# Out-projection weights split beside the narrow products; mix, q and k loaded at other places; the end reordered

## The chip, the cores and the metric

The kernel runs on one core of a Trainium2 chip. The metric is the device time of one execution in microseconds (us); lower is better. The kernel before took 1015.14 us, the median of three runs (1014.92 to 1019.17).

## What is computed

One decoder layer on 1024 positions of width 1024, in float32. The input is normed (`pre_norm_g`) and multiplied by `w_in` (1024 x 7184). The columns of the result feed two groups of heads. The first group is eight heads of differential attention: two causal softmax maps per head, the second subtracted with the weight `lam`, times values of width 128, then a norm and a gate. The second is four heads of gated linear attention (GLA), with decays from a low-rank product, also normed and gated. Both are put side by side and multiplied by `w_out` (2048 x 1024); the result is normed and added to the input:

```
z = einsum('bsd,de->bse', rms_norm(x, pre_g), w_in)
oa = rms_norm(diff_attention(qa, ka, va, lam), subln_g) * (1 - lam_init) * silu(ga)
ob = rms_norm(gla_chunked(qb, kb, vb, log_a), gla_g) * silu(gb)
y = einsum('bse,ed->bsd', concatenate([oa, ob], -1), w_out)
return x + rms_norm(y, post_g)
```

## The kernel before

**Split operands.** Most products are made from float32 operands split in two: ACT copies a tile to a rounded high part, DVE subtracts that from the tile and keeps the low part, and TensorE makes three products, high by high, high by low and low by high. So each weight tile that is used costs one ACT copy and one DVE subtraction. That holds for the weights of the in-projection (L284 with L285, and L327 with L329) and for `w_out`.

**The in-projection in seven products.** Each 1024 x 1024 by 1024 x n product is cut into two by two blocks and made with seven block products instead of eight, numbered 1 to 7; DVE makes the block sums. `order` (L193 to L206) is a list, written by hand, of all these steps, and `go(n)` (L681) does the next n of them: it prepares the weights of the coming steps, issues the matmuls, drains PSUM and hands the result out. There are two kinds of step. A *wide* step (`step_wide`, L442; kinds VB and VA, the values of both attentions) has 24 matmuls of 512 columns into four PSUM banks. A *narrow* step (`step`, L469; a pair `(p, n)` of two 128-column groups) has 12 matmuls into one bank. All 28 wide steps come early, right behind steps 1 and 2 of the first three pairs. Those three pairs keep a bank each through the whole wide stage, so that the wide steps work with five of the eight banks. In a wide step of kind n = 2, 5, 3 or 4 `take_values` (L420) drains the banks: DVE adds (L425), for VA ACT copies the high part (L432) and DVE subtracts (L433), and SP stores the tiles. The staging tiles `st` have four buffers.

**The out-projection's weights.** `w_out` is loaded, split and stored back to DRAM in 32 pieces of 128 x 512, so that later stages can load finished high and low parts. A piece is one load `wo_raw` (L678), an ACT copy `wo_hi`, a DVE subtraction into `wo_raw` and the stores on SP's queue. `wo_raw` has one buffer, so the next load waits until the last store of the piece before has landed. Before the change 17 pieces are done behind wide steps (`wo_wide`, L661: ACT L668, DVE L669, two half tiles each, stores L670 and L671) and 15 behind narrow ones (`wo_step`, L649: ACT L653, DVE L655, stores L657). In the narrow stage a piece's load and its split stand behind steps of certain numbers n, two pieces in seven steps.

**Around the narrow stage.** The low-rank decays are computed between narrow steps: `decay(g)` (L785) is a chain through PE, ACT, DVE, a scan and ACT again. From step (8, 5) on, pieces of GLA are mixed in behind each step (`fill`). `LEAD` steps before the end of `order`, GLA is finished, the first head's q, k and ks (k with its two parts exchanged) are loaded, then the first split `w_out` tiles (`weights(e)`, L1022, into the buffers of h11, h12, s1 and h22, two e to a buffer pair, each free once the last product that reads it is done) and the first two tiles `m_hi`, `m_lo` of GLA's finished part of the mix (`mix`, L1044, into the buffers of s2).

**The attention stage.** Three streams are merged by a fixed plan of costs (`merge`, L1070): scores with softmax (`all_scores`, L1202), values (`all_values`, L1310) and out-projection products that are ready early (`out_early`, L1377). Query blocks go from 7 down to 0 in each head. q, k and ks are tiles of 128 x 2 x 512 in halves 0 and 1. All have one buffer, but for half 0 of k and ks, which have a second one for odd heads (L991). The next head's tiles are loaded behind query block 4. In `values`, `turn` transposes a block of the weights and splits it (ACT L1235, DVE L1236) and `times` (L1239) multiplies.

**The end.** `last_part` (L1354) splits the last head's part of a row tile of the mix (ACT L1357, DVE L1358) and `last_times` multiplies it; `early_ends` (L1462) does that for the first two row tiles, `prime` for the others.

**Queues.** Matmuls are kept in program order. The order on the other engines is set by a scheduler that runs when the program is built. Nearly all DMAs are issued by SP, in one queue; a DMA also waits until the eighth DMA before it on that queue has landed.

## Time and profile before

| what | value |
|---|---|
| median of three runs | 1015.14 us |
| the profiled execution: time, span | 1020.25 us, 1018.6 us |
| mean TensorE clock granted | 0.985 of full |
| busy PE / DVE / ACT / POOL | 973.4 / 740.4 / 594.6 / 141.2 us |
| DMA, mean over the span | 216 GB/s |

The profile page lists the busy time of each engine, the span in 40 slices, the DMA queues and the costliest groups of instructions. Further views of the trace give a table by stretches of time (with the clock granted to TensorE, PEclk), waits by who ended them, instructions in order of time, and the chain of work that ended last. PE is busy in 96% of the span, but a busy PE is not always at its full rate: matmuls overlap in the pipeline, so the count of matmuls in a stretch tells more than its busy time. The stages lie as follows: the input's norm and transposes to 14 us, wide steps with the first narrow ones to 216 us, narrow steps to 649 us (GLA from about 380 to 611 us), attention to about 975 us, then the end.

### The profile page before, as it was taken

To read this page: it belongs to the slowest core of one execution; us is meant where nothing else is said; L and a number is where in the kernel's file an instruction comes from. 1 tells how busy PE (TensorE), PEld (TensorE's weight loads), DVE (VectorE), ACT (ScalarE), POOL (GpSimd) and SP (SyncE) were. 2 spreads that over 40 slices of the span, in tenths; PEclk is the share of its full clock that TensorE was granted. 3 is DMA by queue.
4 is the path that set the end of the run, shared out by engine and by line. 5 is a ranking of instruction groups with operands and counts; after the bars stand their busy time and mean duration, and the time that the engine had idled before them with its cause. 6 is when DMAs were issued, how large, how long until landed. Compare 5 with 4: busy or idle time off the path is not lost.

```text
span 1018.6 us, 14888 instructions
## 1 busy us (share of the span) xinstructions
PE 973.4 (96%) x4866; PEld 814.5 (80%) x4866; DVE 740.4 (73%) x1467; ACT 594.6 (58%) x1169; POOL 141.2 (14%) x153
## 2 busy tenths in 40 slices
PE   6998999799999999999999999899999999999987
PEld 4876767678778888888888888788888888788866
DVE  6995457589879966777777776477777777687745
ACT  8642233335537646765567775256666677677764
POOL 5410000100000000000000000022231222333332
PEclk9999999899989999999999999999999999999999
DMA  9556646586775674566876658995765679964567
GB/s 335 192 144 211 215 154 217 185 233 176 215 244 196 222 265 166 186 197 209 247 207 186 197 186 237 413 328 186 221 202 190 207 251 342 314 179 84 165 198 153
DMA packets 159101, 220.38 MB, mean 216 GB/s; under 512 B 16320, under 2 KB 88256, under 8 KB 158928
## 3 DMA queue, kind: packets, MB, share of 16 engines
q1 hardware_dynamic: 154992, 212.10, 64.5%
q0 software_dynamic: 4032, 7.34, 4.6%
q8 instruction: 38, 0.62, 0.3%
q14 instruction: 39, 0.32, 0.1%
HBM read 133.93 MB, written 88.60 MB: 218 GB/s over the span
## 4 chain that ended last, share of the span: by engine, by line
PE 64%; DMA 12%; DVE 4%; ACT 3%; issue 3%; SPq 1%; POOL 0%; DVEq 0%; ACTq 0%; POOLq 0%
PE x L117 14%; PE z L117 9%; PE ypart L117 9%; PE y L117 8%; PE sc L117 5%; PE po L117 4%; PE yps L117 4%; PE gpo L117 3%; PE v L117 2%; DMA wo_raw<-in_w_out_dram 2%; PE wtr L120 2%; DMA wo_lo<-wo_d 1%; DMA ks<-k_d 1%; DMA q_d<-qk_st 1%; DMA wo_d<-wo_raw 1%
## 5 line engine op out<-in xcount | busy, mean ns | idle before, releaser
L1167 ACT ACTIVATE p<-p,stt 128x896 f32<-128x896 f32 (+7 forms) x128 | 99.4, 777 | 45.4 <-DVE stt L1157 42.2
L329 DVE TENSOR_TENSOR w<-w_raw,w 128x512 fp32r<-128x512 f32 x134 | 91.8, 689 | 38.3 <-ACT w L327 37.8
L327 ACT CAST w<-w_raw 128x512 fp32r<-128x512 f32 x134 | 82.4, 620 | 55.8 <-PE y L117 27.5
L1157 DVE CUSTOM_DVE_ANT_0 p<-sc,maskt 128x512 f32<-128x512 f32 (+3 forms) x128 | 74.7, 585 | 35.2 <-PE sc L117 34.5
L117 PE MATMUL v<-w,s_hi 128*128 128x512 f32 x256 | 83.3, 406 | 14.1 <-DVE v_st L425 12.9
L1193 POOL TENSOR_SCALAR p<-p,stt,lam 128x1024 f32<-128x1024 f32 (+3 forms) x64 | 55.3, 866 | 228.6 <-DVE stt L1192 218.5
L117 PE MATMUL x<-s_hi,w 128*128 128x512 f32 x320 | 82.3, 400 | 3.0 <-ACT s L480 3.0
L117 PE MATMUL ypart<-wo_hi,m_hi 128*128 128x512 f32 x192 | 79.9, 416 | 2.1 <-DMA m_hi<-mixe 1.9
L117 PE MATMUL z<-s_hi,w 128*128 128x512 f32 x320 | 80.5, 394 | 0.2 <-DVE c L491 0.2
L117 PE MATMUL y<-h_hi,w 128*128 128x512 f32 x320 | 80.6, 394 | 0.0
L117 PE MATMUL ypart<-wo_hi,m_lo 128*128 128x512 f32 x192 | 76.3, 397 | 0.7 <-DMA m_lo<-mixe 0.7
L117 PE MATMUL ypart<-wo_lo,m_hi 128*128 128x512 f32 x192 | 75.9, 395 | 0.0
L480 ACT COPY s<-x 128x512 f32<-128x512 f32 x60 | 35.0, 583 | 69.2 <-PE x L117 64.6
L117 PEld LDWEIGHTS x<-s_hi,w 128*128 128x128 f32 x320 | 60.0, 191 | 15.4 <-ACT s L480 3.5
L117 PEld LDWEIGHTS v<-w,s_hi 128*128 128x128 f32 x256 | 49.5, 196 | 28.1 <-DVE v_st L425 15.6
L117 PE MATMUL sc<-k,q 128*128 128x512 f32 (+1 forms) x192 | 71.4, 375 | 0.2 <-DVE stt L1157 0.2
L117 PE MATMUL sc<-ks,q 128*128 128x512 f32 (+1 forms) x192 | 67.3, 353 | 2.2 <-DMA ks<-k_d 2.2
L117 PEld LDWEIGHTS z<-s_hi,w 128*128 128x128 f32 x320 | 59.1, 188 | 12.2 <-DVE c L491 0.6
L117 PEld LDWEIGHTS y<-h_hi,w 128*128 128x128 f32 x320 | 59.0, 188 | 11.7
L117 PE MATMUL v<-w,h_hi 128*128 128x512 f32 x192 | 61.9, 410 | 3.2 <-DVE v_st L425 2.5
L117 PEld LDWEIGHTS po<-wt_hi,v 128*128 128x128 f32 x320 | 54.6, 190 | 7.3 <-ACT wt_hi L1235 1.0
L117 PE MATMUL po<-wt_hi,v 128*128 128x256 f32 (+1 forms) x320 | 59.6, 277 | 0.6 <-ACT wt_hi L1235 0.6
(223 smaller groups left out, 2319.5 us busy)
## 6 DMA issues: line engine op xcount, KB each, us to landing
w_raw<-in_w_in_dram SPq DMA_DIRECT2D x40, 512.0 KB, 4.7
w_block<-in_w_in_dram SPq DMA_DIRECT2D x16, 512.0 KB, 4.9
wo_raw<-in_w_out_dram SPq DMA_DIRECT2D x32, 256.0 KB, 3.1
wo_d<-wo_raw SPq DMA_DIRECT2D x32, 256.0 KB, 2.4
ks<-k_d SPq DMA_DIRECT2D x64, 128.0 KB, 6.0
k<-k_d SPq DMA_DIRECT2D x32, 256.0 KB, 5.4
q<-q_d SPq DMA_DIRECT2D x32, 256.0 KB, 5.1
wo_hi<-wo_d SPq DMA_DIRECT2D x16, 512.0 KB, 7.5
```

The source lines that it names most:

```text
L117: tc.keep_in_program_order(pe.matmul(*a, **k))
L120: tc.keep_in_program_order(pe.transpose(dst, src, ident))
L327: act.copy(w[0], src)
L329: split_last[:] = [dve.tensor_tensor(w[1], src, fp(w[0]), ALU.subtract)]
L480: act.copy(b[k], ps)
L1157: ins = dve.tensor_tensor_reduce(p[:, a:e], sc[:, : e - a], maskt[:, NZ + P - (e - a) :] if last else maskt[:, : e - a], 1.0, 3e38 if i == ...
L1167: act.activation(p[:, :n], p[:, :n], AF.Exp, bias=st[:, m : m + 1], scale=-1.0, accum_out=st[:, 2 + m : 3 + m],)
L1193: pool.tensor_scalar(p1[:, :n], p1[:, :n], st[:, 5:6], lam, ALU.mult, ALU.mult)
```

## The change

Five edits.

1. `wo_wide` is gone. `wo_step` loses its argument and counts its own calls: the first of every three loads a piece, the third splits it. It runs behind every narrow step from (0, 5) on, and not while `quiet` is set, which is the case around decays 2 and 3. All 32 pieces now stand in the narrow stage.
2. The last steps of `order` are rearranged: steps (z, 1) and (z, 2) come ahead of (y, 5). LEAD grows from 8 to 10, `weights` is called four times ahead of four steps, then `mix` twice, then `weights` twice.
3. q half 1 and both halves of k get a second buffer, for odd heads; the next head's q half 1, k and ks half 0 are loaded behind query block 7, only ks half 1 behind block 4.
4. In `times` the two products with the low part of the weights come last.
5. At the end each `last_part` stands one place earlier.

```diff
-    order += [(y, 1), (y, 2), (y - 1, 3), (y, 5), (z, 1), (z, 2), (z, 5), (y, 6), (z, 6), (y, 4)]
+    order += [(y, 1), (y, 2), (y - 1, 3), (z, 1), (z, 2), (y, 5), (y, 6), (z, 5), (z, 6), (y, 4)]
-    LEAD = 8
+    LEAD = 10
...
-    def wo_step(n):
-        if n in (1, 5) and wo_open:
+    wo_n, quiet = [0], []
+
+    def wo_step():
+        wo_n[0] += 1
+        if wo_n[0] % 3 == 0 and wo_open:
             e, dh, raw = wo_open.pop()
             hi = t2k("c", 4, "wo_hi", F32R)
             act.copy(hi, raw)
...
-        if n in (1, 6) and wo_todo:
-            wo_load()
-
-    def wo_wide(more):
...
-        if more and wo_todo:
+        elif wo_n[0] % 3 == 1 and wo_todo:
             wo_load()
...
             if wide(i):
-                if i >= order.index(("VB", 5, 0)):
-                    wo_wide(i + 1 < order.index(("VA", 4, 0)))
                 continue
-            if order[i][0] >= EARLY or order[i][1] > 2:
-                wo_step(order[i][1])
+            if i >= order.index((0, 5)) and not quiet:
+                wo_step()
...
     go(1)
+    quiet.append(1)
     decay(2)
     go(2)
     decay(3)
+    go(1)
+    quiet.clear()
...
-        if h % 2 and half == 0 and n != "q":
-            t = smps[0].tile([P, 2, 512], F32R, tag=f"{n}0", name=f"{n}0")
+        if h % 2 and (n == "k" or (n, half) in (("ks", 0), ("q", 1))):
+            t = smps[0].tile([P, 2, 512], F32R, tag=f"{n}{half}", name=f"{n}{half}")
...
-    for e in range(E, E + 6):
+    for e in range(E, E + 4):
         weights(e)
-    go(2)
+    go(4)
     mix0, mix1 = mix(0), mix(1)
+    weights(E + 4)
+    weights(E + 5)
     go(3)
...
+                if qb == NT - 1 and h + 1 < DA_HEADS:
+                    for n, half in (("q", 1), ("k", 0), ("k", 1), ("ks", 0)):
+                        load_qk(h + 1, n, half)
                 if qb == 4 and h + 1 < DA_HEADS:
-                    for n in ("q", "k", "ks"):
-                        load_qk(h + 1, n, 1)
-                    for n in ("k", "ks"):
-                        load_qk(h + 1, n, 0)
+                    load_qk(h + 1, "ks", 1)
...
-            for t in range(2):
+            for i, t in ((0, 0), (1, 0), (0, 1), (1, 1), (2, 0), (2, 1)):
...
+        last_part(ENDS[0], parts_d[ENDS[0]])
         yield next(carry)
...
-        for st in ENDS[:2]:
-            last_part(st, parts_d[st])
+        for n, st in enumerate(ENDS[:2]):
+            last_part(ENDS[n + 1], parts_d[ENDS[n + 1]])
...
-        last_part(st, parts_d[st])
+        if n > 2:
+            last_part(st, parts_d[st])
```

**Where instructions go on the engines.** The first place is on DVE in the last third of the wide stage, where step VA 5 ends and VA 3 begins; `v` is a PSUM tile, `v_st` its drained copy, `w` a split weight, `w_block` and `w_t` block sums, `s` a kept partial sum. Before:

```order
L462 TENSOR_TENSOR s_1559<-v,s 128x512
L669 TENSOR_TENSOR wo_raw<-wo_raw,wo_hi 128x256 x2
L285 TENSOR_TENSOR w<-w_block,w 128x1024
L425 TENSOR_TENSOR v_st<-v,s_1556 128x512
L425 TENSOR_TENSOR v_st<-v,s_1557 128x512
L669 TENSOR_TENSOR wo_raw<-wo_raw,wo_hi 128x256 x2
L433 TENSOR_TENSOR v_st<-v_st,v_hi 128x512 x2
L285 TENSOR_TENSOR w<-w_block,w 128x1024
L256 TENSOR_TENSOR w_block<-w_block,w_t 128x1024
L425 TENSOR_TENSOR v_st<-v,s_1558 128x512
L425 TENSOR_TENSOR v_st<-v,s_1559 128x512
```

The same place on DVE now, where `wl` and `wd` belong to the low-rank weights:

```order
L462 TENSOR_TENSOR s_1425<-v,s 128x512
L285 TENSOR_TENSOR w<-w_block,w 128x1024
L425 TENSOR_TENSOR v_st<-v,s_1422 128x512
L726 CAST wl_1603<-wd 128x8x16
L726 CAST wl_1603<-wd 128x4x16
L727 TENSOR_TENSOR wl_1603<-wd,wl_1603 128x8x16
L727 TENSOR_TENSOR wl_1603<-wd,wl_1603 128x4x16
L425 TENSOR_TENSOR v_st<-v,s_1423 128x512
L433 TENSOR_TENSOR v_st<-v_st,v_hi 128x512 x2
L285 TENSOR_TENSOR w<-w_block,w 128x1024
L256 TENSOR_TENSOR w_block<-w_block,w_t 128x1024
L425 TENSOR_TENSOR v_st<-v,s_1424 128x512
```

The `wo_raw` subtractions between the drains are gone; four small low-rank instructions stand between the first two drains instead.

The second place is on SP's queue at the end of the narrow stage: `wo8` to `wo13` are the split weights of e = 8 to 13, `q6` and `g7` stores of steps' results, `ks1` and `q0` loads for the first head. Before:

```order
L1031 DMA wo_hi_5688<-wo8_d_131 128x1024
L1031 DMA wo_lo_5689<-wo8_d_131 128x1024
L886 DMA mixe_122<-go_5400 128x4x128 x2
L1001 DMA ks1_5675<-k0_d_93 64x512
L400 DMA g7_d_110<-g_st_5580 128x512
L1001 DMA ks1_5675<-k0_d_93 64x512 x3
L390 DMA q6_d_91<-qk_st_5641 64x512 x2
L390 DMA q6_d_91<-qk_st_5642 64x512 x2
L998 DMA q0_5685<-q0_d_85 128x512 x2
L1031 DMA wo_hi_5692<-wo9_d_132 128x1024
L1031 DMA wo_lo_5693<-wo9_d_132 128x1024
```

The same queue now, from its first such load, and then where the mix follows:

```order
L1021 DMA wo_hi_5586<-wo8_d_131 128x1024
L1021 DMA wo_hi_5590<-wo9_d_132 128x1024
L400 DMA g6_d_109<-g_st_5427 128x512
L390 DMA k6_d_99<-qk_st_5487 64x512 x2
L1021 DMA wo_lo_5587<-wo8_d_131 128x1024
L1021 DMA wo_lo_5591<-wo9_d_132 128x1024
L1021 DMA wo_hi_5594<-wo10_d_133 128x1024
L876 DMA mixe_122<-gg_5329 128x4x128
L1021 DMA wo_lo_5595<-wo10_d_133 128x1024
```

```order
L1021 DMA wo_hi_5680<-wo12_d_135 128x1024
L1021 DMA wo_lo_5681<-wo12_d_135 128x1024
L1021 DMA wo_hi_5684<-wo13_d_136 128x1024
L1021 DMA wo_lo_5685<-wo13_d_136 128x1024
L991 DMA ks1_5573<-k0_d_93 64x512 x4
L1038 DMA m_hi_5672<-mixe_122 128x1024
L1038 DMA m_lo_5673<-mixe_122 128x1024
```

Eight tiles, of e = 8 to 11, now stand ahead of the q6 stores, where two did. On the queue the mix still stands behind all six pairs of weights, as it did before.

The third place is on SP's queue where head 6 begins; the name behind the arrow tells the head (`k6_d` is head 6's k), `v0` and `v1` are its values. Before:

```order
L1108 DMA v0_8617<-v1_d_102 128x1024
L1108 DMA v1_8618<-v1_d_102 128x1024
L1338 DMA m_raw_8721<-mixd_121 128x4x128
L998 DMA k1_8468<-k6_d_99 128x512
L998 DMA q1_8465<-q6_d_91 128x512 x2
L998 DMA k1_8468<-k6_d_99 128x512
L1001 DMA ks1_8471<-k6_d_99 64x512 x4
```

Now:

```order
L1100 DMA v0_8549<-v1_d_102 128x1024
L1100 DMA v1_8550<-v1_d_102 128x1024
L1330 DMA m_raw_8653<-mixd_121 128x4x128
L988 DMA k1_8676<-k7_d_100 128x512
L991 DMA ks1_8411<-k6_d_99 64x512 x4
L988 DMA q1_8670<-q7_d_92 128x512 x2
L988 DMA k1_8676<-k7_d_100 128x512
```

Half 1 of k and q that is loaded here is now that of head 7, a head ahead; head 6's ks1 stands behind one k load instead of four loads.

More of the change, by code (lines that the diff above doesn't have):

```diff
@@ L657, in wo_step @@
                 sp.dma_start(wod[e][t][:, cols(dh)], fp(src))
-        if n in (1, 6) and wo_todo:
-            wo_load()
-    def wo_wide(more):
-        if wo_open:
-            e, dh, raw = wo_open.pop()
-            lo = raw.bitcast(F32R)
-            for c in range(2):
-                hs = slice(c * 256, c * 256 + 256)
-                hi = ap.tile([P, 256], F32R, tag="gu", name="wo_hi", bufs=5)
-                act.copy(hi, raw[:, hs])
-                dve.tensor_tensor(lo[:, hs], raw[:, hs], fp(hi), ALU.subtract)
-                sp.dma_start(wod[e][0][:, dh * 512 + c * 256 : dh * 512 + c * 256 + 256], fp(hi))
-            sp.dma_start(wod[e][1][:, cols(dh)], fp(lo))
-        if more and wo_todo:
+        elif wo_n[0] % 3 == 1 and wo_todo:
             wo_load()
@@ L1240, in times @@
             hi, lo = wt
-            for t in range(2):
+            for i, t in ((0, 0), (1, 0), (0, 1), (1, 1), (2, 0), (2, 1)):
+                a, b = ((v[0], hi), (v[1], hi), (v[0], lo))[i]
                 kt = 2 * g + t
-                end = kt == 2 * j + 1
-                ns = 256 if not end else P
-                for i, (a, b) in enumerate(((v[0], hi), (v[1], hi), (v[0], lo))):
-                    mm(
-                        po[:, 256 - ns :], a[:, kt, :], b[:, 256 * t : 256 * t + ns],
-                        start=(kt == 0 and i == 0), stop=(kt >= 2 * j and i == 2),
-                        skip_group_check=end,
-                    )
+                ns = 256 if kt <= 2 * j else P
+                mm(
+                    po[:, 256 - ns :], a[:, kt, :], b[:, 256 * t : 256 * t + ns],
+                    start=(kt == 0 and i == 0), stop=(kt >= 2 * j and i == 2),
+                    skip_group_check=True,
+                )
         ready = []
```

## The prediction

> **What bounds the kernel now.** I read the page first, then the stretches of time, then who PE waited for, and last the instructions around the longest waits. From the page, the span, the busy time and the slices:
>
> ```profile
> span 1018.6 us, 14888 instructions
> PE 973.4 (96%) x4866; PEld 814.5 (80%) x4866; DVE 740.4 (73%) x1467; ACT 594.6 (58%) x1169; POOL 141.2 (14%) x153
> PE   6998999799999999999999999899999999999987
> ```
>
> PE bounds the kernel, so an edit pays only where it lets PE run at full rate. Busy time hides what is lost. Full rate is read from the chain of waits, where a run of matmuls of 512 columns stands undisturbed; then two tables of stretches, with PE's matmuls as the x behind its busy time and the granted clock as PEclk:
>
> ```profile
> 215.93 2.72 PE z L117 x12
> ```
>
> ```profile
> 75.00:200.00 125.00, 108.51 (x444) 86.23 (x443) 72.27 (x105) 36.43 (x63) 1.69 (x2) 0.95 0.60 196
> 300.00:375.00 75.00, 75.00 (x332) 62.12 (x331) 63.93 (x103) 45.24 (x76) 0.00 (x0) 1.00 0.67 227
> 400.00:525.00 125.00, 125.00 (x678) 107.63 (x677) 90.97 (x147) 79.71 (x142) 3.29 (x4) 1.00 0.69 208
> 645.00:660.00 15.00, 12.45 (x47) 9.55 (x46) 5.29 (x10) 3.32 (x6) 0.00 (x0) 0.89 1.03 412
> 875.00:890.00 15.00, 12.75 (x67) 10.59 (x66) 8.08 (x25) 7.15 (x17) 3.27 (x5) 0.89 1.04 280
> ```
>
> ```profile
> 276.00:301.00 25.00, 21.97 (x85) 17.60 (x84) 21.06 (x38) 10.63 (x19) 0.00 (x0) 0.86 0.79 253
> ```
>
> Twelve matmuls take 2.72 us, 0.2267 each. From 75 to 200 us, wide steps only, 444 matmuls need 100.7 us of the 125: 24.3 us are lost. From 300 to 375 us 332 of them need 75.3: nothing is lost, though the narrow steps there carry pieces of `w_out`. From 276 to 301 us 85 need 19.3, so 5.7 are lost; from 645 to 660 us 47 need 10.7, so 4.3. Around 880 us the matmuls have mixed widths, so there I go by the wait. Who PE waited for, over the whole span (in total, times, longest):
>
> ```profile
> PE v L117 <- DVE v_st L425: 15.4, 6, 6.0
> PE x L117 <- ACT s L480: 3.0, 1, 3.0
> PE sc L117 <- DMA ks<-k_d: 2.2, 1, 2.2
> PE ypart L117 <- DMA m_hi<-mixe: 1.9, 1, 1.9
> PE yps L117 <- ACT m_hi L1357: 1.6, 2, 1.4
> PE v L117 <- DVE w L285: 1.1, 2, 0.6
> PE po L117 <- DVE wt_lo L1236: 0.9, 3, 0.3
> ```
>
> In the wide stage PE waits for drains. What holds DVE, from the waits of 50 to 216 us, and then the longest case in order of time on SP's queue, ACT, DVE and PE:
>
> ```profile
> ACT wo_hi L668 <- DMA wo_raw<-in_w_out_dram: 67.6, 15, 6.8
> DVE wo_raw L669 <- ACT wo_hi L668: 44.7, 13, 6.6
> ```
>
> ```profile
> 182.72 0.42 SPq L671 DMA_DIRECT2D wo_d<-wo_raw  x1
> 184.81 0.33 SPq L678 DMA_DIRECT2D wo_raw<-in_w_out_dram  x1
> ```
>
> ```profile
> 188.69 0.71 ACT L668 CAST wo_hi<-wo_raw 128x256 fp32r<-128x256 f32 x2 [5.63 <-DMA wo_raw<-in_w_out_dram]
> 189.31 1.13 ACT L432 CAST v_hi<-v_st 128x512 fp32r<-128x512 f32 x2
> ```
>
> ```profile
> 183.65 1.28 DVE L425 TENSOR_TENSOR v_st<-v,s 128x512 f32<-128x512 f32 x2
> 189.13 0.76 DVE L669 TENSOR_TENSOR wo_raw<-wo_raw,wo_hi 128x256 fp32r<-128x256 f32 x2 [4.19 <-ACT wo_hi L668]
> 193.44 1.28 DVE L425 TENSOR_TENSOR v_st<-v,s 128x512 f32<-128x512 f32 x2
> ```
>
> ```profile
> 194.17 1.22 PE L117 MATMUL v<-w,s_hi 128*128 128x512 f32 x2 [5.98 <-DVE v_st L425]
> 126.11 0.74 PE L117 MATMUL v<-w,h_hi 128*128 128x512 f32 x2 [2.50 <-DVE v_st L425]
> 128.87 1.05 PE L117 MATMUL v<-w,h_hi 128*128 128x512 f32 x2
> ```
>
> A load that may start only when the last store has landed (184.81) reaches ACT at 188.69. ACT and DVE stand still for it in their own order, with the copies `v_hi` and the drains behind, and the second two banks are drained at 193.44, ten us after the first two. So a piece's DMA round trip sets the pace of the wide steps.
>
> **Part by part.** *The wide stage.* The edit removes 17 pieces: 34 ACT copies, 34 DVE subtractions, and the DMA round trips among them. DVE has 72.27 us of work in 125, pieces included, so without them it has room. Of the 24.3 us, 15.4 + 1.1 are waits; the rest is lost behind the waits, as at 128.87, where a pair takes 1.05 us, 2.8 us after a wait of only 2.50 ended. What can stay: the VA drains form a chain of their own over four staging buffers. Its second two drains need the first two copied (1.13 / 2 us), subtracted, stored and landed; SP needs about 2 us from a store to the next use of its buffer (182.72 to 184.81), so the chain is some 1.28 + 0.6 + 1.3 + 0.5 + 2.1 = 5.8 us, an estimate, and a bank is wanted again one step, 24 x 0.2267 = 5.4 us, after it is full. That is a wait of about 0.4 us, up to 2 where DVE's block sums or, now, the low-rank casts come between; four such places. I leave 4.3 lost (bounds 1 and 14) and take a gain of 20.0. The Trainium skill, TensorE: Matmul & The Clock Gate (Part 1), says the array falls to half its clock only after an idle window of about 3.4 us. By that only the 5.98 us wait could cost more than itself, some 1.7 us by estimate, and 15.4 + 1.1 + 1.7 = 18.2 us would be there to win. Here a wait of 2.50 us was followed by slow matmuls, so the count of matmuls decides, 24.3.
>
> *The narrow stage.* The 17 pieces now add to the 15: about one in three steps instead of two in seven, and so for longer, into the stretch with GLA. Each is a DVE and an ACT instruction that the wide rows give as 0.76 and 0.71 us in halves: 17 x 0.76 = 12.9 us on DVE. It lies beside PE: DVE has 90.97 of 125 us, ACT 79.71, and a piece in three steps (about 10 us with GLA's matmuls) adds some 9 us to each in 125. What is queued behind ACT's wait for a load are the copies that free PSUM banks and that split weights; this row shows such a wait where PE lost nothing:
>
> ```profile
> 357.97 0.62 ACT L653 CAST wo_hi<-wo_raw 128x512 fp32r<-128x512 f32 x1 [3.15 <-DMA wo_raw<-in_w_out_dram]
> ```
>
> Without that cover a stall costs what the next one did, 5.7 us with the slow matmuls behind it. I take 2 us for all (bounds 0 and 12, two stalls).
>
> *The stall at 280 us.* PE waited 3.0 us for a bank that ACT was to free:
>
> ```profile
> 279.51 0.62 ACT L653 CAST wo_hi<-wo_raw 128x512 fp32r<-128x512 f32 x1 [1.26 <-DMA wo_raw<-in_w_out_dram]
> 281.51 0.56 ACT L480 COPY s<-x 128x512 f32<-128x512 f32 x1
> 282.13 3.35 PE L117 MATMUL x<-s_hi,w 128*128 128x512 f32 x7 [3.03 <-ACT s L480]
> ```
>
> This is decay 1, which `quiet` doesn't cover. The scheduler now puts the piece a few instructions earlier on ACT, ahead of the decay's last exponentials, so its wait overlaps theirs. That takes away 1.3 to 3.0 of the wait; I take 3.0 of the 5.7 us (bounds 0 and 5.7).
>
> *Weights and mix.* Before, the first mix tile landed after the last narrow matmul, behind these loads:
>
> ```profile
> 621.84 0.45 SPq L1031 DMA_DIRECT2D wo_hi<-wo_d  x1
> 628.15 2.67 SPq L390 DMA_DIRECT2D q_d<-qk_st  x4
> 631.99 0.43 SPq L1031 DMA_DIRECT2D wo_hi<-wo_d  x1
> 640.98 0.32 SPq L1048 DMA_DIRECT2D m_hi<-mixe  x1
> 642.22 0.32 SPq L1048 DMA_DIRECT2D m_lo<-mixe  x1
> ```
>
> A tile takes 1.24 us of the queue (640.98 to 642.22). The mix is not ahead of the weights on the queue, as the order shows. But six more tiles now stand ahead of the q stores instead of waiting for them from 628 to 632: 6 x 1.24 = 7.4 us less behind them, against a wait of 1.9 us plus 0.7 for the low part. I take 4.0 of 4.3 (bounds 1.9 and 4.3). What is late next is ks half 1, which moved behind the weights; it is wanted only by the first scores, behind the first out-projection products, so it has longer than the mix. The exchanged steps (z, 1), (z, 2) and (y, 5) are the same matmuls and cost nothing by themselves.
>
> *Head 6.* PE waited 2.25 us for ks, and the clock stood at 0.89 for 15 us, 1.65 us more. Before head 6's ks stood k and q, four loads; now one. Four loads of 256 KB at 280 GB/s, the rate of that stretch, are 3.7 us; three less give 2.8, more than the wait. I take 2.25 + 1.65 = 3.9 (bounds 0, if the queue is as late by then, and 3.9). The three loads don't vanish: head 7's stand there instead, behind ks, and nobody waits for them for a head. The second buffers cost memory alone.
>
> *End and `times`.* Waits for `m_hi` (1.6) and `wt_lo` (0.9) are what can go: the copies of `last_part` are issued one row tile ahead, and the two products that need the late low part stand behind four that don't. The instructions are the same ones. I take 2.0 (bounds 0 and 2.5).
>
> Sum: 20.0 + 3.0 + 4.0 + 3.9 + 2.0 - 2.0 = 30.9 us. The profiled execution took 1020.25 us (1.65 outside the span) and would take 989.4. The median stands 5.1 us below it, so the forecast for it is 1015.1 - 30.9 = 984.
>
> **The rivals.** *Banks, not pieces, hold the wide steps* (0.14). The waits end at `v_st`, and three early pairs hold three banks, so the drains may stay late without the pieces. For it: the chain above has no slack. Against: DVE's 44.7 us of waiting for `wo_hi`. Half of the 24.3 stays: gain 12 instead of 20, time 992; with the decay stall unchanged too, 995.
>
> *The pieces take their waits along* (0.10). ACT and DVE still meet each load in their own order, now 32 times, beside GLA's copies. Place: ACT at `wo_hi` in the narrow stage; price 5.7 us each, as at 280 us. Three such stalls give 984 + 17 = 1001; six give 1018; from seven of 32 the kernel is slower than before, eight give 1030. Against it: 15 such pieces cost PE one stall before. The Trainium skill's same page (Part 1, on queue depths) has ACT and DVE as strict first in, first out, which is the ground for this rival; the trace agrees, with `v_hi` held 5.63 us behind `wo_hi`.
>
> *The mix edit doesn't do what it says* (0.06). The queue keeps six pairs of weights ahead of it; if the first ones wait for their buffers as before, the 4.0 us stay: 988.
>
> **How the numbers follow.** The forecast has 0.70, with its own range of 975 to 993: all bounds at their good end give 23.3 + 5.7 + 4.3 + 3.9 + 2.5 = 39.7, that is 975, and 15 us in the wide stage with 6 lost in the narrow one give 993. The range over the cases is 973 to 1001, which takes in the first and last rival and the second with up to three stalls; the 2 us below 975 are for the spread of the runs, 4 us in three. A measurement of this kernel can tell about 0.5%, 5 us, from no change. Faster by more has 0.92. Within 0.5% is 0.04 (four to six stalls), slower 0.04 (seven or more); these come from the second rival alone and from what I may have missed.
>
> **What would show it.** Right: no ACT wait for `wo_raw` and no PE wait over 2 us between 75 and 200 us, the wide steps done by about 195 us; 32 casts of 128x512 between there and 530 us with PE at 110 matmuls in 25 us; no wait for `m_hi<-mixe` or `ks<-k_d` over 0.5 us. Wrong: PE waits for `v_st` of over 8 us in total, waits for ACT `s` in the narrow stage, or PE waiting for a split weight w there.

## The result and the profile after

The changed kernel takes 1009.66 us (median of 9 runs, 1003.63 to 1011.7) where the kernel before, timed beside it, takes 1018.23 (9 runs, 1014.34 to 1019.81). The ratio is 0.9923 [0.99, 0.9946]: 0.8% faster, some 8 us, where 31 were forecast and a range of 973 to 1001. The direction was right; three quarters of the gain are missing. The profiled execution took 1008.7 us.

From the page of the changed kernel, and its stretches of time (us, then each engine's busy time with instructions, the clock, the DMA share and GB/s):

```profile
span 1007.0 us, 14819 instructions
...
PE 964.5 (96%) x4866; PEld 810.5 (80%) x4866; DVE 737.1 (73%) x1450; ACT 589.9 (59%) x1152; POOL 141.7 (14%) x153
...
PE   6999999999899999999979999979999999999997
```

```profile
75.00:200.00 125.00, 124.89 (x551) 102.16 (x551) 83.71 (x111) 36.71 (x48) 2.74 (x5) 1.00 0.47 141
200.00:350.00 150.00, 143.85 (x622) 117.06 (x621) 124.80 (x209) 79.72 (x137) 0.00 (x0) 0.98 0.70 221
350.00:600.00 250.00, 241.26 (x1275) 205.86 (x1275) 183.22 (x299) 163.91 (x295) 6.56 (x8) 0.99 0.77 239
...
640.00:700.00 60.00, 53.16 (x275) 45.10 (x276) 34.86 (x99) 29.11 (x63) 8.91 (x10) 0.94 0.81 278
```

The wide stage now runs at full rate: 551 matmuls in its 125 us, 444 before. The later stretches don't: at 0.2267 us each, 622 matmuls need 141 of the first 150 us. What PE waits for has changed (total, times, longest):

```profile
PE gms L117 <- DVE gqd L967: 7.9, 3, 5.9
PE po L117 <- ACT wt_hi L1227: 7.3, 2, 6.7
PE x L117 <- ACT s L480: 6.1, 3, 4.3
PE yps L117 <- ACT yps L1480: 1.0, 1, 1.0
PE ypart L117 <- ACT yst L1366: 1.0, 2, 0.7
```

The waits for `v_st`, ks and `m_hi` are gone from the list. The first two rows name waits that the kernel before did not have over 1 us; the third was one wait of 3.0.

To add up what PE loses, waits and slow matmuls together, I took for each matmul of a trace the time from its start to the start of the next, less the median of that for its shape, and summed it by stretch (us lost; the profiled execution of each kernel):

| kernel | 0–75 | 75–200 | 200–600 | 600–640 | 640–700 | 700–850 | 850–900 | 900–end | all |
|---|---|---|---|---|---|---|---|---|---|
| before | 7.7 | 24.6 | 8.3 | 0.0 | 5.9 | 4.9 | 5.4 | 6.8 | 63.5 |
| changed | 6.8 | 0.3 | 22.8 | 1.8 | 10.2 | 3.5 | 1.7 | 4.9 | 52.0 |

The wide stage gave back nearly all it lost. Two stretches lose more: the narrow steps 14.5 us, and the first attention head, 10.2 from 640 to 700, where before 5.0 of the 5.9 stood at the waits for mix: without those, 9.3 more. Mix itself loses 1.8 instead of 5.0, and the other stretches 7.9 less.

**The narrow steps.** ACT (first fence), SP's queue (second) and PE (third) around two waits in the changed kernel, the one from 273.5 to 277.8 us and the one from 507.9 to 513.9 us:

```profile
267.52 0.62 ACT L656 CAST wo_hi<-wo_raw 128x512 fp32r<-128x512 f32 x1 [4.95 <-DMA wo_raw<-in_w_out_dram]
...
276.68 0.62 ACT L656 CAST wo_hi<-wo_raw 128x512 fp32r<-128x512 f32 x1 [6.98 <-DMA wo_raw<-in_w_out_dram]
277.20 0.58 ACT L480 COPY s<-x 128x512 f32<-128x512 f32 x1
...
506.67 0.62 ACT L656 CAST wo_hi<-wo_raw 128x512 fp32r<-128x512 f32 x1 [2.55 <-DMA wo_raw<-in_w_out_dram]
507.20 0.63 ACT L961 ACTIVATE sq<-go 128x512 f32<-128x512 f32 x1
```

```profile
269.01 0.45 SPq L660 DMA_DIRECT2D wo_d<-wo_raw  x1
...
272.48 0.33 SPq L667 DMA_DIRECT2D wo_raw<-in_w_out_dram  x1
```

```profile
254.16 2.11 PE L117 MATMUL x<-s_hi,w 128*128 128x512 f32 x8 [0.92 <-ACT s L480]
...
277.84 3.78 PE L117 MATMUL x<-s_hi,w 128*128 128x512 f32 x8 [4.34 <-ACT s L480]
...
513.85 0.76 PE L117 MATMUL gms<-gqd,ones 128*128 128x512 f32 x1 [5.92 <-DVE gqd L967]
```

Read it as a ring. The cast at 267.52 lets the low half be stored (269.01); the next load may start when that has landed (272.48), and the next cast begins at 276.68: 9.2 us for one turn. A piece in three steps asks for one every 3 x 2.72 = 8.2 us. So here the ring is the slower of the two, and the lateness adds up: the five casts from 240.8 to 276.7 us stand 8.6 to 9.2 us apart, and ACT's wait ahead of them grows from 3.0 to 6.98 us, with the copy `s` that PE waits for behind the last. PE's stall gives the ring time to catch up, and the next casts wait for nothing. Beside GLA the turn is longer (13.3 us from the cast at 493.4 to that at 506.67), and so are the steps. At 507 us the cast stands ahead of GLA's squares (`sq`), which go ACT, DVE, ACT, DVE, ACT, DVE before PE may take the mean. All ACT waits for these loads:

```profile
L656 ACT CAST wo_hi<-wo_raw 128x512 fp32r<-128x512 f32 x32 | 19.8, 619 | 72.0 <-DMA wo_raw<-in_w_out_dram 64.8 <-DVE w L329 4.1 <-DMA q_d<-qk_st 3.0
```

In the kernel before, the casts of the wide stage waited 67.6 us, and those of the narrow one:

```profile
ACT wo_hi L653 <- DMA wo_raw<-in_w_out_dram: 10.6, 8, 3.2
```

So the edit moved the waiting, 78.2 us before and 64.8 now, and removed little of it.

**The first head.** ACT, SP's queue and PE in the changed kernel:

```profile
656.66 0.57 ACT L1366 COPY yst<-ypart 128x512 f32<-128x512 f32 x1
...
676.29 0.58 ACT L1366 COPY yst<-ypart 128x512 f32<-128x512 f32 x1 [9.78 <-DMA y_d<-yst]
676.77 0.48 ACT L1227 CAST wt_hi<-wtr 128x384 fp32r<-128x384 f32 x1
```

```profile
657.60 0.86 SPq L988 DMA_DIRECT2D q<-q_d  x2
658.51 1.96 SPq L988 DMA_DIRECT2D k<-k_d  x4
660.51 4.76 SPq L991 DMA_DIRECT2D ks<-k_d  x4
665.44 1.21 SPq L1100 DMA_DIRECT2D v<-v_d  x2
...
669.73 0.32 SPq L1380 DMA_DIRECT2D y_d<-yst  x1
```

```profile
677.31 1.12 PE L117 MATMUL po<-wt_hi,v 128*128 128x256 f32 x4 [6.75 <-ACT wt_hi L1227]
...
678.65 0.73 PE L117 MATMUL ypart<-wo_hi,m_hi 128*128 128x512 f32 x1
```

Both `yst` buffers are written by 657.2, but their stores stand on SP behind the loads for head 1; the first is issued at 669.73 and landed at 676.2. ACT's third copy waits for it 9.78 us, the cast `wt_hi` stands behind the copy, and PE waits 6.75 us and runs slow after it.

### The profile page after: what moved, and what is told of

It reads as the page before. It is cut to its first block, busy times and chain, and to the rows that moved or that the text cites. A ratio compares the mean times of both kernels' runs of the same rounds, so it can differ in the third digit from the quotient of the medians.

```text
span 1007.0 us, 14819 instructions
## 1 busy us (share of the span) xinstructions
PE 964.5 (96%) x4866; PEld 810.5 (80%) x4866; DVE 737.1 (73%) x1450; ACT 589.9 (59%) x1152; POOL 141.7 (14%) x153
## 4 chain that ended last, share of the span: by engine, by line
PE 65%; DMA 17%; DVE 9%; issue 3%; ACT 3%; SPq 1%; POOL 0%; DVEq 0%; ACTq 0%; POOLq 0%
PE v L117 14%; PE ypart L117 10%; PE x L117 9%; PE sc L117 6%; PE y L117 6%; PE z L117 5%; PE po L117 5%; DMA wo_d<-wo_raw 4%; DMA wo_raw<-in_w_out_dram 4%; PE yps L117 3%; PE wtr L120 3%; PE gpo L117 2%; DMA ks<-k_d 2%; DMA wo_lo<-wo_d 1%; DMA q_d<-qk_st 1%
## 5 line engine op out<-in xcount | busy, mean ns | idle before, releaser
L117 PE MATMUL v<-w,s_hi 128*128 128x512 f32 x256 | 79.3, 390 | 0.6 <-DVE w L285 0.5
L284 ACT CAST w<-w_block 128x1024 fp32r<-128x1024 f32 x24 | 25.1, 1052 | 66.3 <-PE v L117 41.7
L256 DVE TENSOR_TENSOR w_raw<-w_raw 128x512 f32<-128x512 f32 x80 | 55.7, 696 | 11.1 <-DMA w_raw<-in_w_in_dram 10.1
L656 ACT CAST wo_hi<-wo_raw 128x512 fp32r<-128x512 f32 x32 | 19.8, 619 | 72.0 <-DMA wo_raw<-in_w_out_dram 64.8
L908 POOL TENSOR_SCALAR_AFFINE_SELECT gan<-gan 128x512 f32<-128x512 f32 x8 | 6.6, 820 | 387.8 <-ACT gan L907 387.8
L117 PE MATMUL v<-w,h_hi 128*128 128x512 f32 x192 | 59.8, 399 | 0.4 <-ACT h_hi L574 0.4
```

What stands on the lines that cost most here:

```text
L117: tc.keep_in_program_order(pe.matmul(*a, **k))
L256: dve.tensor_tensor(dst, a, b, ALU.subtract)
L284: act.copy(w[0], src)
L656: act.copy(hi, raw)
L908: pool.affine_select(a, a, [[0, 4], [1, P]], ALU.is_ge, 0.0, base=0, channel_multiplier=-1)
```

## The experiments

My theory: two new things took back some 24 us (14.5 and 9.3 by the table), the loads of the moved pieces in the narrow steps, and the early loads of head 1 ahead of the first y stores. The rivals: the narrow stage loses by transfers or by the work of the pieces, or because it starts 24 us sooner; the stall in head 0 comes from the mix or from the order of the last steps. All runs are timed beside the kernel before, and the ratios are to it. What PE lost by stretch, in the same way as above (`all` includes the stretches that are not shown):

| run | us | ratio, 95% | 75–200 | 200–600 | 600–640 | 640–700 | 850–900 | all |
|---|---|---|---|---|---|---|---|---|
| direct | 1007.07 | 0.9908 [0.9887, 0.9928] | 4.0 | 1.8 | 1.3 | 9.4 | 1.9 | 49.4 |
| direct_held | 991.87 | 0.9757 [0.9731, 0.9782] | 0.3 | 5.8 | 1.7 | 10.2 | 1.8 | 34.1 |
| pieces_alone | 1010.26 | 0.9940 [0.9918, 0.9963] | 0.3 | 20.9 | 3.4 | 4.0 | 2.4 | 51.3 |
| mix_end | 1012.51 | 0.9962 [0.9939, 0.9985] | 22.8 | 7.0 | 0.0 | 5.9 | 5.5 | 58.6 |
| qk_alone | 1018.49 | 1.0019 [0.9998, 1.0039] | 21.8 | 5.3 | 0.0 | 12.0 | 4.5 | 63.5 |
| qk_undone | 1005.68 | 0.9903 [0.9876, 0.9931] | 0.2 | 20.7 | 1.5 | 4.6 | 2.1 | 44.2 |
| head0_late | 1006.03 | 0.9892 [0.9871, 0.9914] | 0.2 | 22.9 | 1.3 | 7.4 | 1.7 | 48.8 |
| v_late | 1005.21 | 0.9890 [0.9869, 0.9912] | 0.2 | 22.1 | 2.1 | 7.0 | 1.9 | 47.7 |
| lo_apart | 1004.83 | 0.9895 [0.9868, 0.9922] | 0.2 | 19.5 | 0.3 | 9.8 | 1.7 | 47.6 |
| combo | 997.59 | 0.9819 [0.9787, 0.9852] | 0.2 | 13.7 | 0.9 | 4.5 | 5.0 | 40.3 |
| lo_four | 995.69 | 0.9787 [0.9758, 0.9816] | 0.2 | 3.3 | 7.8 | 8.7 | 1.6 | 37.3 |
| four_in_place | 1001.34 | 0.9849 [0.9825, 0.9874] | 0.2 | 10.7 | 15.8 | 2.1 | 1.8 | 45.4 |
| best | 993.76 | 0.9773 [0.9743, 0.9802] | 0.2 | 3.2 | 7.0 | 7.7 | 1.8 | 34.9 |
| best_two | 990.43 | 0.9757 [0.9731, 0.9783] | 0.2 | 10.0 | 1.6 | 5.6 | 2.5 | 33.6 |

### Are the pieces the cause in the narrow steps?

`direct` leaves the split out: SP copies each piece from `w_out` to both of its places in DRAM.

```diff
-        if wo_n[0] % 3 == 0 and wo_open:
...
-        elif wo_n[0] % 3 == 1 and wo_todo:
-            wo_load()
+        if wo_n[0] % 3 == 0 and wo_todo:
+            e, dh = wo_todo.pop(0)
+            for t in range(2):
+                sp.dma_start(wod[e][t][:, cols(dh)], w_out[0, e * P : (e + 1) * P, cols(dh)])
...
```

> The changed kernel with the 32 pieces of w_out taken off ACT and DVE: SP copies each piece of w_out as it is to both parts (so the low part isn't a remainder: the split is left out), one piece in three narrow steps as before. Theory A (the moved pieces took their waits along): the narrow stage loses 22 us in the changed kernel, 7 of them around the first decays; without the pieces at most 4 are left from 250 to 550 us, no wait for `gqd` or ACT `s` is over 1 us, and the time is 18 us lower: 992. Theory B (the narrow stage and GLA now meet differently because the wide steps end 24 us sooner; the pieces are bystanders): the waits at 273 and 507 us stay, and the time is within 4 us of the changed kernel, 1006 to 1010. If only the one at 273 us goes, 1003.

The waits between 253 and 514 us went, but the time did not: a copy that waits for no buffer was issued as soon as SP was free. SP's queue, and PE's waits from 40 to 76 us, in `direct`:

```profile
25.91 24.65 SPq L656 DMA_DIRECT2D wo_d<-in_w_out_dram  x28
51.07 0.92 SPq L220 DMA_DIRECT2D w_early<-in_w_in_dram  x2
```

```profile
PE x L117 <- DVE s L619: 7.7, 1, 7.7
PE v L117 <- ACT w L284: 6.5, 1, 6.5
```

The loads of weights stood behind 28 copies, and the first 200 us lost 20 us more than in the changed kernel. So the run says where the waits come from, but nothing by its total. `direct_held` puts each copy behind the last store of its own step (the lines that record that store are left out here):

```diff
+            with tc.issue_after(stores[0].ins):
                 for t in range(2):
                     sp.dma_start(wod[e][t][:, cols(dh)], w_out[0, e * P : (e + 1) * P, cols(dh)])
```

> As `direct` (the pieces of w_out off ACT and DVE, the split left out), but each copy on SP now stands behind the last store of its own stage, so that none runs ahead to 19 to 70 us as it did there (16 us lost between 50 and 75 us). Theory A (the pieces' casts on ACT and what is queued behind them cost the narrow stage 22 us): 50 to 75 us loses under 1 us again, 250 to 550 us loses at most 3, the head-0 stall stays, and the time is 16 to 20 us below the changed kernel's: 990 to 993. Theory B (the narrow stage loses its time to transfers, which are as many here): 250 to 550 us loses over 8 us, 1000 or more.

991.87, inside the 990 to 993 of theory A; from 200 to 600 us 5.8 us are lost, 17 less than in the changed kernel, and the ratio is lower by 0.9923 - 0.9757 = 0.0166, the same 17 us. The bytes written are the same, so the transfers alone (B) are not the cause, and the narrow steps start as early as in the changed kernel, so that is not it either. A's bound of 3 us from 250 to 550 us was missed (5.7): one wait for `gqd` (2.1 us, with slow matmuls behind it) stayed at 497 us, with no piece on ACT or DVE. It is the same matmul that waits 5.92 us in the changed kernel, so not all of that wait is the pieces'.

### Waiting or work?

`lo_apart`:

```diff
-            lo = raw.bitcast(F32R)
+            lo = t2k("c", 4, "wo_lo", F32R)
...
+            if wo_todo:
+                wo_load()
-        elif wo_n[0] % 3 == 1 and wo_todo:
+        elif not wo_open and wo_todo:
```

> The changed kernel with the low half of a piece written to a staging buffer of its own, so that the next load needn't wait for a store, and is asked for together with the cast before it, three steps ahead instead of two. Same copies and subtractions, one staging buffer more in use. Theory A1 (ACT's wait for the load is what costs): ACT's waits for `wo_raw` fall from 72 us to under 20, the waits of PE for ACT `s` and `gqd` go, 12 to 18 us less: 992 to 998. Theory A2 (the work itself, 0.6 us of ACT and 0.8 of DVE a piece, and its place among the other copies is what costs): ACT's waits fall as much, but 250 to 550 us still loses over 10 us, and the time is within 5 us of the changed kernel's. Mishap: `c` waits for the store of the low half (waits of DVE at L491), a new stall in the place of the old.

Neither as stated: ACT's waits fell to 29 us, not to A1's 20, and the loss only to 19.5; the time and the loss are nearer to A2. Some of the waits that were left stood in a bad place, ahead of ACT's last link of the squares, and PE waited 5.07 us for them at 511 us (ACT in `lo_apart`):

```profile
507.37 0.62 ACT L656 CAST wo_hi<-wo_raw 128x512 fp32r<-128x512 f32 x1 [1.73 <-DMA wo_raw<-in_w_out_dram]
507.90 0.61 ACT L327 CAST w<-w_raw 128x512 fp32r<-128x512 f32 x1
508.42 0.62 ACT L968 CAST gqd<-sq 64x512 fp32r<-64x512 f32 x1
```

`lo_four` is `lo_apart` with one number moved:

```diff
-        if wo_n[0] % 3 == 0 and wo_open:
+        if wo_n[0] % 4 == 0 and wo_open:
```

> As `lo_apart` (low half in a buffer of its own, the next load asked for together with the cast), but a piece every fourth narrow step, not every third: the same 32 pieces, spread over 128 steps. Theory A1 (what PE loses is ACT's wait for the load, and what stands behind it; it fell from 72 us to 29 there but hit the chain of squares at 500 us): with a fourth step of lead ACT waits under 12 us for `wo_raw`, and 250 to 550 us loses under 8 (20 in `lo_apart`): 10 to 13 us below `lo_apart`, 992 to 996. Theory A2 (the work and its place do): as many casts on ACT, so only a fourth less is lost, 1000 or more.

995.69, inside A1's range. By A2 a quarter of the 19.5 would have gone; 3.3 are left. From 200 to 350 us DVE and ACT do 217 and 142 instructions in `lo_four` and 215 and 142 in `lo_apart`, with 13 casts of pieces against 16, and the loss there falls to 0.6 us. So at this spacing the work of the pieces is hidden, and ACT waits 7.7 us for their loads up to 560 us. The total of those waits, 17.1, misses A1's 12: the last two pieces now reach the tail, where SP holds the loads for attention (PE in `lo_four`, at 616 us):

```profile
PE z L117 <- DVE c L491: 4.9, 1, 4.9
```

`four_in_place` moves that spacing in the changed kernel alone, with the low half in place:

```diff
-        if wo_n[0] % 3 == 0 and wo_open:
+        if wo_n[0] % 4 == 0 and wo_open:
...
-        elif wo_n[0] % 3 == 1 and wo_todo:
+        elif wo_n[0] % 4 == 1 and wo_todo:
```

> The changed kernel with one number moved: a piece every fourth narrow step, not every third (load at the first, cast at the fourth: three steps of lead, the low half still in place, so one step for its store). If the lead alone is what costs (theory A1): ACT waits under 25 us for `wo_raw` (72 in the changed kernel, 8 in `lo_four`), 250 to 550 us loses under 6, and the stall of the last pieces near 616 us comes as in `lo_four`: 995 to 999. If the store of the low half ahead of each load matters as much: ACT waits 30 us or more, 1000 to 1004.

1001.34 is in its second case, but in part because the late pieces in the tail cost more than expected (PE waits 4.4 and 7.6 us for `c`, and the stretch loses 15.8 against 7.8 in `lo_four`). The narrow steps show it better: from 200 to 600 us 10.7 are lost, so the spacing, with one more step of lead, gives 12 of the 19.5 that `lo_four` gives, and the buffer, with one more step again, the rest. The store ahead of the load matters as well. One thing stays open: up to 560 us ACT waits about as long for loads here (28.2 us) as in `lo_apart` (29.2), and yet `lo_apart` loses 19.5. Either its waits stand in worse places, or the thinner spacing helps by itself; no run separates the two.

### What holds the first head?

`qk_undone` puts `load_qk` and its calls back as they were:

```diff
-        if h % 2 and (n == "k" or (n, half) in (("ks", 0), ("q", 1))):
+        if h % 2 and half == 0 and n != "q":
```

> The changed kernel with the buffers and loads of q, k, ks as in the kernel before. Theory A (the early loads of head 1 stand ahead of the y stores on SP's queue and so hold ACT's copy into `yst`): the wait of PE for `wt_hi` at 670 us (6.7) and the slow matmuls after it go, 8 us between 650 and 700; the wait for ks at head 6 comes back, 3.9 us. Net 4 us faster than the changed kernel: 1005 to 1006. Theory B (the stall in head 0 comes from the order at the end of the narrow stage or from mix and weights, not from these loads): it stays, and with the wait for ks back the time is 1013 to 1014.

Theory A, in part: the loss there fell from 10.2 to 4.6, but a wait of 2.1 us for `wt_hi` stayed, and the wait for ks at head 6 hardly came back (0.7 us). That the time, 1005.68, is the one that A gave is luck: it had counted 8 us won in head 0, where the trace has 5.6, and 3.9 lost at head 6, where it has 0.4. `head0_late` moves the loads of head 1 alone:

```diff
-                if qb == NT - 1 and h + 1 < DA_HEADS:
+                if qb == NT - 1 and 0 < h < DA_HEADS - 1:
...
-            sp.dma_start(yd[0][dh], y_tile(ps[dh]))
+            first = sp.dma_start(yd[0][dh], y_tile(ps[dh]))
+        with tc.issue_after(first.ins):
+            for n, half in (("q", 1), ("k", 0), ("k", 1), ("ks", 0)):
+                load_qk(1, n, half)
```

> The changed kernel with one thing moved: for head 1 alone the early loads of q half 1, k half 0 and 1, and ks half 0 (nine DMAs) are issued behind the two stores of the first row tile's products. Theory A (these loads delay the y stores): the wait for `wt_hi` at 670 us goes and no other comes, 7 to 9 us less: 1000 to 1002. Theory B (some other work is late in head 0): the wait stays over 4 us, and the time is within 3 us of the changed kernel's. Mishap: the scores of head 1 then wait for the loads, which PE would show as a wait for k_d or q_d after 690 us.

The wait for `wt_hi` fell to 0.6 us, but the mishap came, and the time (1006.03) misses A's 1000 to 1002: head 1's scores are wanted from 673.6 us.

```profile
PE sc L117 <- DMA ks<-k_d: 3.1, 1, 3.1
```

`v_late` moves the two loads of v for head 1 behind those stores (`y_first` holds the last of them), and leaves q and k:

```diff
...
-            if h + 1 < DA_HEADS:
+            if h and h + 1 < DA_HEADS:
                 nxt = load_v(h + 1)
             yield from values(h, 2, v, o[1])
+            if not h:
+                with tc.issue_after(y_first[0].ins):
+                    nxt = load_v(1)
...
```

> The changed kernel with one thing moved: the two loads of v for head 1 (1 MB) stand behind the first row tile's two y stores on SP, not ahead of them; the early loads of q and k stay ahead. In `head0_late` it was the q and k loads, and PE then waited 3.1 us for ks. Theory A (what stands ahead of the y stores decides, in bytes): 1 MB less ahead of them, at some 400 GB/s, brings them 2.6 us earlier; the wait for `wt_hi` falls from 6.7 to some 4 us and the slow matmuls behind it with it: 3 to 4 us less than the changed kernel, 1005 to 1006. Theory B (the queue's limit of DMAs under way decides, not the bytes): two DMAs of the seventeen ahead make under 1 us, 1008 to 1010.

The wait for `wt_hi` is 3.7 us instead of 6.7 and the time 1005.21, as A has it. The two edits that put work into this place, each alone on the kernel before: `qk_alone` has the third edit only,

> The kernel before with the third edit alone: second buffers for q half 1 and k half 1 of odd heads, and the loads placed early. The prediction gave it 3.9 us. Theory A (it trades the wait for ks at head 6 against a wait in head 0, where its four loads of q and k stand ahead of the first y stores): the wait for ks (2.2) goes, a wait of PE for `wt_hi` of 3 to 5 us comes near 672 us, with slow matmuls behind it; together 0 to 3 us slower than the kernel before. Theory B (the stall in head 0 needs the earlier mix of the second edit): no wait for `wt_hi` over 1 us, 3 to 4 us faster.

and `mix_end` the second, fourth and fifth.

> The kernel before with the second, fourth and fifth part alone: mix ahead of half the weights, the exchanged steps and the longer tail, the order of the last products and copies. The prediction gave them 4.0 + 2.0 us. The wait for `m_hi` at 648 us goes and that for its low half stays: 2 to 3 us there; the end gives 2 to 2.5. Theory A (out-projection then runs earlier in head 0 and meets the y stores behind the same loads): a wait for `wt_hi` of about 2 us appears near 680 us, as in `qk_undone`; together 2 to 4 us faster. Theory B (that wait belongs to the moved pieces): none, 5 to 6 us faster.

PE's waits in `qk_alone` (first) and in `mix_end`:

```profile
PE po L117 <- ACT wt_hi L1235: 4.9, 2, 4.4
PE sc L117 <- DMA ks<-k_d: 3.1, 1, 3.1
```

```profile
PE po L117 <- ACT wt_hi L1237: 2.5, 2, 1.9
PE sc L117 <- DMA ks<-k_d: 2.4, 1, 2.4
```

Both make the stall by themselves, 4.4 and 1.9 us, and 6.7 together: the one puts more ahead of the stores, the other lets the row tile want them sooner (in `mix_end` the second `yst` copy stands at 664.1 us, in the kernel before at 670.0). Which part of `mix_end` does that, the mix or the order of the last steps, no run separates. `four_in_place` agrees from the other side: PE comes to head 0 late there, and the stretch loses 2.1. And the third edit alone does not remove the wait for ks, which the prediction gave it as its gain. SP's queue in the kernel before (first) and in `qk_alone`:

```profile
866.48 0.32 SPq L998 DMA_DIRECT2D k<-k_d  x1
...
872.76 3.52 SPq L1001 DMA_DIRECT2D ks<-k_d  x4
```

```profile
868.94 0.32 SPq L998 DMA_DIRECT2D k<-k_d  x1
870.22 4.91 SPq L1001 DMA_DIRECT2D ks<-k_d  x4
```

ks now goes first, 2.5 us earlier than before, but the four take longer on the queue and the wait is 3.1 us. In the changed kernel the queue reaches ks at 862.67 and nobody waits. Without the third edit the wait is 0.7 us in `qk_undone`, 1.0 in `pieces_alone` and 2.3 in `combo` (below). So something other than this edit moves it, and what that is stays open.

### The parts and the sum

`pieces_alone` is the first edit on the kernel before:

> The kernel before with the first edit alone: all 32 pieces in narrow steps, one in three, quiet around decays 2 and 3; mix, q/k/ks and the end stay as before. Theory A (the edit wins 24 us in the wide steps and pays some 15 in the narrow ones): 8 to 11 us faster than the kernel before, some 1006 to 1010, with no wait over 1 us from 75 to 200 us and the wait for `gqd` near 507 us. Theory B (most of what was lost in the changed kernel's narrow stage comes from the other edits, the order of the last steps among them): 18 us faster or more, below 1000.

Theory A, with 6 us instead of 8 to 11. The three parts add: (0.9940 - 1) + (0.9962 - 1) + (1.0019 - 1) = -0.0079, and the changed kernel has -0.0077. Each of them is known to some 0.002, so the agreement is closer than it had to be.

### A better version

`combo` joins `lo_apart`, `qk_undone` and `v_late`:

> The changed kernel with three mends: the low half of a piece in a buffer of its own (`lo_apart`), the buffers and loads of q, k, ks as before (`qk_undone`), and v of head 1 behind the first y stores (`v_late`). If the three losses are separate and A1 holds, they add: some 14 us in the narrow stage, 6 in head 0 and 2 for v, less 1 at head 6: 988 to 994, 2 to 2.5% faster than the kernel before. If a loss mended only shows the next one late, 998 to 1003.

997.59: between its two cases. `lo_apart` was half a mend, and waits for q and ks in head 1 (1.2 and 1.1 us) and for ks at head 6 (2.3) came. `best` takes the pieces as in `lo_four`, the old q and k loads for head 1 alone, and v of head 1 behind the first store of the second row tile:

```diff
-        if h % 2 and (n == "k" or (n, half) in (("ks", 0), ("q", 1))):
+        if h % 2 and ((n == "k" or (n, half) in (("ks", 0), ("q", 1))) if h > 1 else half == 0 and n != "q"):
...
```

> The changed kernel with the mends together: pieces as in `lo_four`; for head 1 alone the buffers and loads of q, k, ks as in the kernel before, for the later heads as in the changed one; v of head 1 behind the first y store of the second row tile. Stalls gone: 12 to 18 us in the narrow stage, 7 to 9 in head 0, and the wait for ks at head 6 stays away. 982 to 988. If v is then late (a wait of PE for v near 740 us) or the narrow stage keeps its losses, 990 to 998.

993.76, in the second of its cases: the stall of the last pieces stayed (4.4 us at 620 us), and v of head 0 was waited for (2.7 us). `best_two` casts two pieces in seven steps, so that they end in time:

```diff
-        if wo_n[0] % 3 == 0 and wo_open:
+        if wo_n[0] % 7 in (0, 3) and wo_open:
```

> As `best`, with the pieces two in seven narrow steps (leads of three and four steps in turn), so that the last one is cast near 540 us and not behind the loads of the tail. If the stall at 616 us (4.4 us, 6 with what follows) was those last pieces, it goes; if three steps of lead are too few beside GLA, 2 to 6 us come back at 440 to 510 us. 986 to 990 if only the first holds, 991 to 994 if both do.

990.43, ratio 0.9757 [0.9731, 0.9783], just above the first of its cases: the stall at 616 us is gone. From 200 to 600 us 10.0 are lost against 3.2 in `best`, but no late load of a piece shows there: DVE was late with `c` at 242 us because it stood at a small load of `lam` (last row below), and the wait for `gqd` at 502 us, 1.9 us, is the one that `direct_held` has without pieces (2.1). It is 2.4% faster than the kernel before and 1.7% faster than the changed one; against `best` the difference lies within the intervals. From its page and its waits:

```profile
span 988.9 us, 14856 instructions
...
PE 959.8 (97%) x4866; PEld 808.0 (82%) x4866; DVE 738.3 (75%) x1450; ACT 591.0 (60%) x1152; POOL 141.7 (14%) x153
```

```profile
PE po L117 <- ACT wt_hi L1234: 2.9, 2, 2.3
PE z L117 <- DVE c L491: 2.8, 1, 2.8
PE gms L117 <- DVE gqd L969: 2.4, 2, 1.9
...
DVE lam L820 <- DMA lam<-in_lambda_k_dram: 4.0, 2, 3.2
```

## Why the prediction was right in sign and wrong in size

By the table, the sum of 30.9 became 11.6, 19.3 less. The narrow steps are 15.5 us short of their terms (-2.0 and +3.0 against -14.5) and the first head 10.1 short of its (+4.0 against -6.1); the rest did 6.3 better than forecast. So two steps failed, the first of them the larger.

- **Wide stage, +20.0: right, and forecast a little too small.** 24.6 lost before, 0.3 after. The banks did not hold the steps, so that rival falls.
- **Narrow stage, -2.0 with bounds 0 and 12: the step that failed.** Measured are 14.5 more lost than before, and 17 from the pieces by `direct_held`. The prediction never set the turn of the one buffer (cast, store landed, load, next cast) against the interval at which the new place asks for it. It put the overlap down to the busy share of DVE and ACT, and to one row where a wait of 3.15 us cost nothing, at the older pace of two in seven, 3.5 x 2.72 = 9.5 us. It took three steps for about 10 us, which holds beside GLA; ahead of it they are 8.2. A turn of some 9 us keeps the pace of 9.5 and not that of 8.2. The casts of the wide stage alone would not have told: there they stand 5.6 to 10.6 us apart. The rival "the pieces take their waits along" had the mechanism, the place and about the price; it deserved far more than 0.10.
- **The stall at 280 us, +3.0: it came, for the reason given as far as this trace shows.** Matmuls are kept in program order, so the same matmul can be found by counting: the one that waited 3.03 us at 282.13 stands at 254.16 in the changed kernel and waits 0.92, and the cast (249.83) now stands ahead of the decay's exponentials (250.97 and 252.06). The 5.7 us lost there became 1.1. It isn't steady, however: in `qk_undone`, with the same narrow edit, that matmul waits 3.72 us. The wait of 4.34 us up to 277.84 is a new one, 84 matmuls later, where the kernel before had none; it belongs to the step above.
- **Weights and mix, +4.0: about right in itself.** The waits for mix fell from 5.0 to 1.8 us lost (3.2). The sentence on what is late next named ks half 1; what was late next were the y stores, and that cost more than was won.
- **Head 6, +3.9: the number came by luck.** 3.7 less is lost there in the changed kernel, but the edit alone does not do it (`qk_alone`, 3.1 us of waiting), and most of it comes without the edit (`qk_undone`).
- **"The second buffers cost memory alone": the other step that failed.** The prediction followed the moved loads at heads 6 and 7 only. At head 0 the same lines put four DMAs more ahead of the first y stores; with the earlier mix that cost some 9 us between 640 and 700.
- **End and `times`, +2.0: right, and forecast a little too small.** 1.9 us less are lost from 900 us on and 1.4 less from 700 to 850.

The terms of the table: 24.3 - 14.5 - 6.1 (600 to 700) + 3.7 + 3.3 + 0.9 = 11.6 us between the two profiled executions. The medians differ by 8.6: the profiled execution of the kernel before was one of its slower ones, that of the changed kernel was not.

The Trainium skill's page TensorE: Matmul & The Clock Gate (Part 1, on queue depths) has ACT as strict first in, first out. The rows at 276.68 and 277.20 agree: the copy `s` starts only after the cast that waited 6.98 us.

## What to carry to other kernels

Before a job with one buffer is moved to another stage, work out its turn (store landed, load, next use) from rows and set it against the interval at which the new place asks for it; if the turn is longer, the wait grows from use to use until something stalls, whatever the busy shares say. Where an edit moves loads in a loop over heads, follow them at the first head too: what they overtake on the queue there may be a store that frees a buffer. And a moved wait costs by what is queued behind it: 3.15 us cost PE nothing in the kernel before, while 2.55 us stood ahead of a chain for which PE waited 5.92 (2.12 without the pieces).

When a trace is set against an earlier one, find the same matmul by its place in program order. Here the clock time led astray: the stalls at 282 us before and at 278 us after are different ones.

## What the hardware showed beside that

Some waits of 2 to 3 us were followed by slow matmuls, others were not. In `best_two` a wait of 2.35 us (second row) is followed, two us later, by matmuls of 0.63 us (third) where the same form took 0.40 before (first):

```profile
655.78 0.40 PE L117 MATMUL ypart<-wo_hi,m_hi 128*128 128x512 f32 x1
...
659.46 0.68 PE L117 MATMUL po<-wt_hi,v 128*128 128x256 f32 x4 [2.35 <-ACT wt_hi L1234]
...
661.37 0.63 PE L117 MATMUL ypart<-wo_hi,m_hi 128*128 128x512 f32 x1
```

The slow ones last from 661.2 to 664.7 us, 3.5 us in which the granted clock is 0.51, so the wait of 2.35 us cost some 4. The length of the wait alone does not tell, however: after 2.72 us (kernel before, at 98.7 us) and after 3.13 us (`qk_alone`, at 882.4) the granted clock did not fall.

The Trainium skill's page TensorE: Matmul & The Clock Gate (Part 1) puts the fall to half clock behind an idle window of about 3.4 us. In `best_two` the idle time was shorter, and the measurement decides.
